# Moving the modulation's dot products in a two-layer trunk kernel: none amid layer 0's attention, the second norm's beside the output projections, the second gate's by columns in the down stage

## The chip, the cores and the metric

The kernel runs on one core of one Trainium2 chip. The metric is the device time of one execution in microseconds (us); less is better. The engines are TensorE (PE, matmuls; PEld is its loading of weights), VectorE (DVE), ScalarE (ACT), GpSimd (POOL) and SyncE (SP, which here issues most loads from HBM). Each engine works through its own instructions in order and waits at semaphores for the others.

## The reference

Two decoder layers over 512 tokens of 1024 channels, in float32. Six vectors per layer, made from a conditioning vector c, shift, scale and gate the two halves of a layer:

```python
mod = (c_act @ w_ada + b_ada)[:, None, :]
sh1, sc1, g1, sh2, sc2, g2 = jnp.split(mod, 6, axis=-1)
h = rmsnorm(x, norm1_w) * (1 + sc1) + sh1
u = h @ w_in                      # pool, conv, q/k/v and the gates' logits
...                               # pool mixer, short convolution, block-sparse attention
merged = (gates[:, :, 0] * (y_pool @ p_pool)
          + gates[:, :, 1] * (y_conv @ p_conv)
          + gates[:, :, 2] * (y_attn @ p_attn))
x = x + g1 * (merged @ w_out)
h2 = rmsnorm(x, norm2_w) * (1 + sc2) + sh2
x = x + g2 * ((jax.nn.silu(h2 @ w_gate) * (h2 @ w_up)) @ w_down)
```

So SC1 and SH1 are wanted at a layer's first norm, G1 at the output projections' residuals, SC2 and SH2 at the second norm, and G2 at the residuals of the down projection.

## The kernel before

Activations lie features by tokens: eight tiles (KT = 8) of 128 features x 512 tokens. Every product is made from split numbers. A float32 tile is divided into a high half (an ACT activation, `whi` for weights in L327, `big` for activations in L514) and a low half (a DVE subtraction, `wlo` in L330, `big` in L515), and `mm3` (L159) issues three matmuls per 128x128 block: high by high, high by low, low by high, which for an activation's use in a projection means: the weight's high half with the activation's high and low half, and the weight's low half with the activation's high half.

A layer runs in stages. First the input projections (L755 on); then attention with pool and convolution chains; then three sets of gates; then, in the order of the list `GATE2` (L75), the last gates and the attention's projection: a step `attn j` makes four block products into a PSUM bank, `gated` (L936, recorded as L938) multiplies them by the gate, L972 adds the other branches, and `split_from` (L510) splits the result into `merged[j]`. `tail` (L981) then runs the output projections: for each of the output columns n the eight merged tiles are multiplied by weight blocks, `residual` (L977, recorded as L978) scales the column by the modulation's gate and adds it to x, and the second norm's sums of squares are taken. Just ahead of `tail`, `table` (L172, recorded as L174) runs a one-column activation with the next function, ahead of which ACT loads the function's table. Then comes the feed-forward network in four parts (`PARTS`, L47): gate and up products, partly in pairs with fewer multiplications (`glu_pair`), followed by the part's down projection, again in eight columns with a residual each. Layer 0's part 3 ends with `tail` and layer 1's first norm.

A modulation vector is made of eight **dots**: one 512 KB tile of `w_ada` is loaded by SP, and one DVE instruction (`ada_dot`, L374, recorded as L376) multiplies it, 128x1024, by the activated c and accumulates a column of `mod`. `ada_end` (L405) adds the bias to all eight columns, and for SC1 and SC2 folds in the norm's weight. There are 96 dots. The 16 first ones are written out at the start; the others are queued as tasks in `bulk` by `ada_tasks` (L413).

What sets the order: a clock counted in matmul columns (`tick`, L135, called by `mm3`) runs queued tasks at `bulk_rate` per tick; `flush_bulk` runs all that are left and `drain` ends pending generators. So tasks take their place in the engines' orders when the program is built, between whatever is issued at that point. `ada_step` (L398) issues load and dot together; the tile comes from the pool tag `w4` (six slots, shared with the weights that POOL sums) or, with `early=True`, from `raw`, the ring of RAW = 3 tiles that weight loads use too. A load's issue waits on SP until the slot is free, and later loads wait behind it; a scheduler puts the issue of a load earlier than its dot.

Where the dots lie before the change:
- layer 0: SC2 and SH2 (`early`) amid the attention, at rate 0.27, the rest flushed after the last `attn` step; G2 in the output projections of both layers at rate 0.9;
- the next layer's vectors as list `later`, a part of it in each down stage of layer 0: `DOTS` = 8, 8 and 2 tasks in parts 0 to 2, five in part 3, and what is left in layer 1's first stage at rate 0.75 (L763 on).

Of the kernel before, what the change touches and what calls it, by code (L numbers as in the profile page):

```python
# [25 lines left out]
KT = D // P  # L26
# [21 lines left out]

SUMS_AHEAD = 4

DOTS = (8, 8, 2, 0)

RAW, BIG = 3, 46

# [25 lines left out]
def hybrid_trunk(ctx, tc, xT, ws, ada, cols, pool_w, qk_w, crow, pos, con, out):  # L80
# [50 lines left out]
    def flush_bulk():  # L131
        while bulk:
            bulk.popleft()[1]()
# [12 lines left out]
    def drain():  # L146
        while fibers:
            tick()
# [256 lines left out]
    def ada_end(l, part):  # L405
# [4 lines left out]
        if part == G1:  # L410
            V.tensor_scalar(m, m, 0.5, None, op0=ALU.mult)

    def ada_tasks(l, parts, early=False):  # L413
        out = []
        for part in parts:
            for j in range(KT):
                out.append((1.2, lambda part=part, j=j: ada_step(l, part, j, early)))
            out.append((0.2, lambda part=part: ada_end(l, part)))
        return out
# [320 lines left out]
    for l in range(L):  # L740
# [7 lines left out]
        for n, (k, lo, hi) in enumerate([(k, 0, S) for k in range(KT)] if l == 0 else HALVES + REST):  # L748
            if l == 0:
                if k + 3 < KT:  # L750
                    first.append(ada_first_load(k + 3))
                if k + 2 < KT:
                    ada_first(k + 2, first[k + 2], SC1)
                    ada_first(k + 2, first[k + 2], SH1)
                    norm.first_scaled(k + 2)  # L755
                    norm.first_hi(k + 2)
                loaded.append(load_w())
                if k + 2 < KT:
                    norm.first_lo(k + 2)
            if k not in held:  # L760
                held[k] = next_w(0 if l == 0 else None)
            if l > 0 and n == 1:
                second(norm, l, 0, bank)  # L763
                bulk.extend(later)
                bulk_rate[0] = 0.75
            w = held[k]
            h = norm.k(k)
            for t in range(lo // P, hi // P):
                mm3(q_ps[t], cut(h, slice(None), slice(t * P, (t + 1) * P)), wrow(w, 0), k == 0, k == KT - 1)
            for z in range(3):  # L770
                mm3(f_ps[z][:, lo:hi], wblk(w, 4 + z), cut(h, slice(None), slice(lo, hi)),
                    k == 0 and lo == 0, k == KT - 1)
# [148 lines left out]
            mm3(pp, (pw["h"][:, j, :], pw["l"][:, j, :]), pooled[j], True, True)  # L921
            y_pool.append(split_from(pp, scale=col(C_PS + j)))

        if l == 0:
            bulk.extend(ada_tasks(l, (SC2, SH2), True))
        bulk_rate[0] = 0.27
        ahead_now[0] = 3

        def gate():
# [29 lines left out]
        for step, j in GATE2:  # L959
            if step == "gate":  # L960
                sg2[j] = gate()
                continue
            if j == 0:
                drain()
            if j % 2 == 0:
                aw_ = next_w()
            p1 = ps_mm()
            for z in range(PAIRS):
                mm3(p1, wblk(aw_, 4 * (j % 2) + z), y_attn[z], z == 0, z == PAIRS - 1)
            t = sg2.pop(j)  # L970
            gated(t, p1)
            V.tensor_add(t, t, m01[j])  # L972
            merged.append(split_from(t))
        flush_bulk()


        def residual(k, src, lo, hi, part):  # L977
# [50 lines left out]
            return go  # L1028

        ahead_now[0] = 4  # L1030
        bulk.extend(ada_tasks(l, (G2,)))
        bulk_rate[0] = 0.9
        n2 = Norm()
        n2.h = [bigt(F32) for _ in range(KT)]
        table(AF.Abs_reciprocal_sqrt, t[:, 0:1])
# [41 lines left out]
        def glu_pair(last):  # L1077

            both = range(2)
            e = [ps_pair()[:, 0, :BLOCK] for _ in both]  # L1080
            a, c = [None] * 2, [None] * 2
            one, two = [None] * 2, [None] * 2
            w = [next_w() for _ in both]
            for z in both:
                group(e[z], w[z], 1, "B21", True)
            for z in both:
                a[z], one[z] = ps_mm()[:, :BLOCK], tmp()
                group(a[z], w[z], 0, "B11", True)
                C11 = one[z][:, :BLOCK]
                A.activation(C11, a[z], AF.Copy)  # L1090
                V.tensor_add(C11, C11, e[z])
            w = [next_w() for _ in both]
            for z in both:
                c[z], two[z] = ps_mm()[:, :BLOCK], tmp()
                group(c[z], w[z], 0, "R1", True)
                A.activation(two[z][:, BLOCK:], c[z], AF.Copy)
            for z in both:
                group(a[z], w[z], 1, "-V", False)
                A.activation(one[z][:, BLOCK:], a[z], AF.Copy)

            w = [next_w(2 if last else None) for _ in both]
            for z in both:
                group(c[z], w[z], 0, "B22", False)
                C12 = one[z][:, BLOCK:]
                V.tensor_add(C12, C12, c[z])
            for z in both:
                group(a[z], w[z], 1, "T3", False)
                m22 = two[z][:, BLOCK:]
                ins = V.tensor_add(m22, m22, a[z])
                if last:  # L1110
                    pin(ins)
            w = next_w(2 if last else None)
            for z in both:
                group(a[z], w, z, "T4", False)

            (g1, u1), (g2, u2) = one, two
            A.activation(g1, g1, AF.Silu)
            A.activation(g2[:, BLOCK:], g2[:, BLOCK:], AF.Silu, scale=-1.0)
            A.activation(g2[:, :BLOCK], a[0], AF.Silu, scale=-1.0)
            V.tensor_mul(u1, u1, g1)  # L1120
            act.append(split_from(u1))
            V.scalar_tensor_tensor(u2[:, BLOCK:], u2[:, BLOCK:], -1.0, g2[:, BLOCK:], op0=ALU.mult, op1=ALU.mult)
            V.scalar_tensor_tensor(u2[:, :BLOCK], a[1], -1.0, g2[:, :BLOCK], op0=ALU.mult, op1=ALU.mult)
            act.append(split_from(u2))
            dots_after[0] = last_split[0]

        for part, (along, single, pairs) in enumerate(PARTS):
            act = []
            nk = along + single + 2 * pairs
            if along:  # L1130
                held = {}
                for n, (k, lo, hi) in enumerate(HALVES + REST):
                    if n == 1:
                        second(norm, l, 1, bank)
                        table(AF.Silu, norm.y[:, 0:1])
                    if k not in held:
                        held[k] = next_w(3 if n == 0 else None)
                    for z in range(2 * FA):
                        mm3(f_ps[z][:, lo:hi], wblk(held[k], z), cut(norm.k(k), slice(None), slice(lo, hi)),
                            k == 0 and lo == 0, k == KT - 1)  # L1140
                    if k >= HK:
                        make_forms(k - HK)
                del held
                for z in range(FA):
                    glu(f_ps[z], f_ps[FA + z])
            for _ in range(single):
                wg = next_w()
                g = ps_mm()
                feature_tile(g, wg)
                u = ps_mm()  # L1150
                feature_tile(u, next_w())
                glu(g, u)
            bulk_rate[0] = 0.0
            for p in range(pairs):
                glu_pair(p == pairs - 1)
            if l + 1 < L:
                if part == 0:
                    later = ada_tasks(l + 1, (SC1, SH1, SC2, SH2))
                n = DOTS[part]
                bulk.extend(later[:n])  # L1160
                del later[:n]
            bulk_rate[0] = 1.5
            blk = Blocks(nk, 4)
            if part + 1 < len(PARTS):
                for n in range(KT):
                    if n == KT // 2:
                        bulk_rate[0] = 0.0
                    o = ps_mm()
                    for k in range(nk):
                        mm3(o, blk(n, k), act[k], k == 0, k == nk - 1)  # L1170
                    residual(n, o, 0, S, G2)
            elif l + 1 == L:
                tail(lambda k: act[k], blk, G2, nk, None, True)
            else:
                flush_bulk()
                drain()
                bulk.extend(later[:5])
                del later[:5]
                bulk_rate[0], credit[0] = 0.8, 0.0
                n1 = Norm()  # L1180
                table(AF.Abs_reciprocal_sqrt, f32(act[-1][1])[:, 0:1])
                scratch = ps_pair()
                bank = scratch[:, 1]
                tail(lambda k: act[k], blk, G2, nk, n1, False, lead(n1, l + 1, 0, bank), 4)
                norm = n1
# [100 lines left out]
```

## Time and profile before

| | us |
|---|---|
| median of three runs (lowest to highest) | 1452.05 (1451.97 to 1452.85) |
| profiled execution | 1453.0 |
| its span | 1451.2 |
| PE busy in the span | 1442.0 |
| DVE busy | 1063.1 |
| ACT busy | 663.5 |
| the 80 dots on `w4`, busy on DVE | 95.9 |

The clock granted to PE was 1.00 throughout. A row of the timeline gives the start in us, the duration, the engine, the line, the operation with its output and input, and how many instructions in a row it stands for (then the duration is from the first one's start to the last one's end); in brackets stand the idle time before it and what ended it. Instructions of one engine can overlap by a little: the next starts before the end of the one before. A row of the groups ends with busy time, mean, and the engine's idle time just before them with the releaser.

### The profile page before, as it was taken

The numbers are of one execution on the slowest core, as the hardware profiler recorded it, in microseconds if no ns is written. First come the engines' busy times: TensorE is split into PE (matmuls) and PEld (weight loads), VectorE is DVE, ScalarE is ACT, GpSimd is POOL, SyncE is SP. The second block draws the span as 40 slices with busy tenths as digits, with TensorE's granted clock in tenths as the row PEclk, the third lists the DMA queues.
The fourth block names the chain that finished last, engine by engine and source line by source line (L and its number), as shares of the span: only waits on it lengthen the run. The fifth ranks groups of instructions, "written<-read, shape, count | busy, mean of one in ns | idle before, by whom it ended". The sixth has DMA issues, their size and how long they took to land.

```text
span 1451.2 us, 21838 instructions
## 1 busy us (share of the span) xinstructions
PE 1442.0 (99%) x8379; PEld 1264.8 (87%) x8379; DVE 1063.1 (73%) x1879; ACT 663.5 (46%) x1138; POOL 105.2 (7%) x157
## 2 busy tenths in 40 slices
PE   9999999999999999999999999999999999999998
PEld 7888788888988998989988877888889989989997
DVE  7987888858686767677797776776577757657663
ACT  4634555533553452535444355555335525534450
POOL 0000000001100311210000000000020102111200
PEclk9999999999999999999999999999999999999999
DMA  9644333364436767756545422223473436636432
GB/s 352 223 141 167 124 115 104 117 217 152 100 132 213 196 174 205 187 153 195 190 147 178 151 87 73 73 73 109 153 200 90 135 113 175 174 106 185 131 92 83
DMA packets 84409, 217.18 MB, mean 150 GB/s; under 512 B 10832, under 2 KB 23760, under 8 KB 84304
## 3 DMA queue, kind: packets, MB, share of 16 engines
q1 hardware_dynamic: 67456, 177.37, 35.9%
q0 software_dynamic: 16128, 37.76, 11.8%
q8 instruction: 65, 1.06, 0.3%
q10 hardware_dynamic: 720, 0.66, 0.1%
q14 instruction: 40, 0.33, 0.1%
HBM read 213.65 MB, written 2.10 MB: 149 GB/s over the span
## 4 chain that ended last, share of the span: by engine, by line
PE 92%; DVE 5%; DMA 1%; ACT 1%; issue 1%; SPq 0%; ACTq 0%; DVEq 0%
PE mm L151 78%; PE pair L151 12%; PE mm L157 1%; DVE wlo L330 1%; DMA w<-in_ada 1%; DVE w L376 0%; DVE raw L376 0%; DMA x<-in_xT 0%; DMA raw<-in_ws 0%; DVE tmp L643 0%; DVE asm L622 0%; ACT tmp L638 0%; DVE asm L629 0%; DVE asm L623 0%; ACT tmp L635 0%
## 5 line engine op out<-in xcount | busy, mean ns | idle before, releaser
L151 PE MATMUL mm<-big,whi 128*128 128x512 f32 (+1 forms) x4362 | 1080.2, 339 | 1.7 <-DVE big L938 0.9
L151 PEld LDWEIGHTS mm<-big,whi 128*128 128x128 f32 x4362 | 745.2, 190 | 87.2 <-DVE big L938 1.5
L151 PE MATMUL mm<-big,wlo 128*128 128x512 f32 (+1 forms) x2181 | 736.1, 338 | 0.0
L151 PEld LDWEIGHTS mm<-big,wlo 128*128 128x128 f32 x2181 | 413.8, 190 | 44.5
L327 ACT ACTIVATE whi<-raw 128x1024 fp32r<-128x1024 f32 (+2 forms) x240 | 248.9, 1040 | 265.7 <-PE mm L151 190.2
L330 DVE TENSOR_TENSOR wlo<-raw,whi 128x1024 fp32r<-128x1024 f32 (+2 forms) x240 | 283.9, 1192 | 50.5 <-ACT whi L327 47.7
L327 ACT ACTIVATE whi<-w 128x1024 fp32r<-128x1024 f32 x72 | 76.2, 1058 | 148.1 <-PE mm L151 85.3
L978 DVE SCALAR_TENSOR_TENSOR x<-mm,mod,x 128x512 f32<-128x512 f32 (+1 forms) x90 | 61.7, 689 | 78.1 <-PE mm L151 77.9
L256 POOL DMA_DIRECT2D w<-in_ws x72 | 46.3, 656 | 951.6 <-issue 294.1
L330 DVE TENSOR_TENSOR wlo<-w,whi 128x1024 fp32r<-128x1024 f32 x72 | 86.7, 1221 | 31.6 <-ACT whi L327 30.9
L376 DVE SCALAR_TENSOR_TENSOR w<-w,csil 128x1024 f32<-128x1024 f32 x80 | 95.9, 1220 | 16.9 <-DMA w<-in_ada 16.8
L151 PE MATMUL pair<-whi,big 128*128 128x512 f32 x224 | 76.8, 390 | 0.0
L258 POOL DMA_DIRECT2D w<-in_ws x72 | 64.0, 897 | 157.8 <-DMA w<-in_ws 142.6
L151 PE MATMUL pair<-big,whi 128*128 128x256 f32 (+1 forms) x376 | 74.0, 294 | 0.0
L151 PEld LDWEIGHTS pair<-big,whi 128*128 128x128 f32 x376 | 60.4, 191 | 2.2
L151 PE MATMUL mm<-whi,big 128*128 128x512 f32 x160 | 57.2, 394 | 1.4 <-ACT big L501 1.1
L151 PE MATMUL pair<-big,wlo 128*128 128x256 f32 (+1 forms) x188 | 55.3, 294 | 0.0
L938 DVE SCALAR_TENSOR_TENSOR big<-big,mm 128x512 f32<-128x512 f32 x48 | 32.5, 683 | 28.6 <-PE mm L151 28.5
L151 PEld LDWEIGHTS pair<-whi,big 128*128 128x128 f32 x224 | 42.1, 188 | 8.8
L515 DVE TENSOR_TENSOR big<-tmp,big 128x512 fp32r<-128x512 f32 x48 | 33.1, 691 | 21.4 <-ACT big L514 20.4
L514 ACT ACTIVATE big<-tmp 128x512 fp32r<-128x512 f32 x48 | 29.9, 622 | 36.2 <-DVE tmp L1120 12.8
L151 PE MATMUL pair<-wlo,big 128*128 128x512 f32 x112 | 43.6, 390 | 0.0
(190 smaller groups left out, 1238.5 us busy)
## 6 DMA issues: line engine op xcount, KB each, us to landing
raw<-in_ws SPq DMA_DIRECT2D x146, 512.0 KB, 3.3
w<-in_ada SPq DMA_DIRECT2D x80, 512.0 KB, 4.9
w<-in_ws POOLq DMA_DIRECT2D x144, 256.0 KB, 4.7
raw<-in_ws SPq DMA_DIRECT2D x64, 256.0 KB, 3.8
raw<-in_ws SPq DMA_DIRECT2D x24, 384.0 KB, 3.5
raw<-in_ada SPq DMA_DIRECT2D x16, 512.0 KB, 3.3
raw<-in_ws SPq DMA_DIRECT2D x16, 448.0 KB, 5.1
raw<-in_ws SPq DMA_DIRECT2D x36, 128.0 KB, 2.8
```

Source lines behind the costliest of these rows:

```text
L151: tc.keep_in_program_order(T.matmul(*a, **k))
L157: tc.keep_in_program_order(T.transpose(*a))
L256: nc.gpsimd.dma_start(dst, self.source(0, 1))
L258: nc.gpsimd.dma_start(dst, self.source(*other), accum_op=ALU.add)
L327: A.activation(hi[:, :n], raw[:, :n], AF.Copy)
L330: ins = V.tensor_sub(lo[:, :n], raw[:, :n], f32(hi)[:, :n])
L376: return V.scalar_tensor_tensor(aw, aw, 1.0, csil, op0=ALU.mult, op1=ALU.mult, accum_out=mod[l][:, part, j:j + 1])
L514: A.activation(hi, src, AF.Copy)
L515: last_split[0] = V.tensor_sub(lo, src, f32(hi))
L938: V.scalar_tensor_tensor(sg, sg, 1.0, branch, op0=ALU.add, op1=ALU.mult)
L978: V.scalar_tensor_tensor(x[k][:, lo:hi], src, mod[l][:, part, k:k + 1], x[k][:, lo:hi], op0=ALU.mult, op1=ALU.add)
```

## The change

- `DOTS` becomes (0, 9, 4, 0), and `later` holds only SC1 and SH1 of the next layer: part 0's down stage of layer 0 has none of the next layer's tasks, parts 1 and 2 have nine and four, part 3 what is left (five), and layer 1's first stage none.
- No dots are queued amid layer 0's attention (rate 0). In both layers SC2's and SH2's tasks are queued at the first `attn` step, at rate 0.85 and on the `w4` ring; the flush after the last `attn` step goes, so that what is left runs on into the output projections, where `tail` flushes it.
- G2's tasks in the output projections go. Instead `g2_column` makes one column of G2: its load, its dot, and a one-column ACT activation that adds the bias. In part 0's down stage of both layers three columns are made ahead of the loop over the output columns and column n + 3 at the top of iteration n, so that four stand ahead of the first column's products.

In the resulting order, DVE has four dots in a row behind the split of the last pair's product and ahead of the three splits of down weights that followed it before. Between `attn 4` and `attn 7` two dots stand on DVE: one between the low halves of merged tiles 4 and 5, one behind the next weight tile's low half. On ACT the table load and its one-column activation stand between the high halves of merged tiles 6 and 7, in both layers; before, they stood behind both. PE's order is the same instruction by instruction. Lines behind L413 move by two to seven: L514/L515 become L520/L521, L938 becomes L940, L972 becomes L976, L978 becomes L981.

```diff
-DOTS = (8, 8, 2, 0)
+DOTS = (0, 9, 4, 0)
...
+    def g2_column(l, j):
+
+        ada_step(l, G2, j, False)
+        m = mod[l][:, G2, j:j + 1]
+        A.activation(m, m, AF.Identity, bias=colt[:, l, C_ADA + G2 * KT + j:C_ADA + G2 * KT + j + 1])
...
             if l > 0 and n == 1:
                 second(norm, l, 0, bank)
-                bulk.extend(later)
-                bulk_rate[0] = 0.75
...
-        if l == 0:
-            bulk.extend(ada_tasks(l, (SC2, SH2), True))
-        bulk_rate[0] = 0.27
+        bulk_rate[0] = 0.0
...
             if j == 0:
                 drain()
+                bulk.extend(ada_tasks(l, (SC2, SH2)))
+                bulk_rate[0] = 0.85
...
             merged.append(split_from(t))
-        flush_bulk()
...
         ahead_now[0] = 4
-        bulk.extend(ada_tasks(l, (G2,)))
-        bulk_rate[0] = 0.9
...
                 glu_pair(p == pairs - 1)
+            if part == 0:
+                for j in range(3):
+                    g2_column(l, j)
             if l + 1 < L:
                 if part == 0:
-                    later = ada_tasks(l + 1, (SC1, SH1, SC2, SH2))
+                    later = ada_tasks(l + 1, (SC1, SH1))
...
                     if n == KT // 2:
                         bulk_rate[0] = 0.0
+                    if part == 0 and n + 3 < KT:
+                        g2_column(l, n + 3)
...
-                bulk.extend(later[:5])
-                del later[:5]
+                bulk.extend(later)
                 bulk_rate[0], credit[0] = 0.8, 0.0
```

## The prediction

> **What bounds the kernel now.** I read the page first: the span, the engines, the chain of work that ended last, the dots and their loads; its last row here is from the view of the dots' operand (us of DVE's idle time, times).
>
> ```profile
> span 1451.2 us, 21838 instructions
> PE 1442.0 (99%) x8379; PEld 1264.8 (87%) x8379; DVE 1063.1 (73%) x1879; ACT 663.5 (46%) x1138; POOL 105.2 (7%) x157
> PE 92%; DVE 5%; DMA 1%; ACT 1%; issue 1%; SPq 0%; ACTq 0%; DVEq 0%
> L376 DVE SCALAR_TENSOR_TENSOR w<-w,csil 128x1024 f32<-128x1024 f32 x80 | 95.9, 1220 | 16.9 <-DMA w<-in_ada 16.8
> w<-in_ada SPq DMA_DIRECT2D x80, 512.0 KB, 4.9
> ...
> DMA w<-in_ada: 16.8, 14
> ```
>
> TensorE (PE) is busy for 1442.0 of 1451.2 us, and 92% of the chain is its own matmuls. The change touches none of them: PE runs the same matmuls in the same order in both kernels. So only PE's waits can change, and the second question is how much waiting there is to win. I asked for PE's waits in the stretch of layer 0's attention (which has dots amid it) and in the same stretch of layer 1 (which has none), and for both stretches' busy times.
>
> ```profile
> PE mm L157 <- DVE tmp L672: 0.6, 1, 0.6
> PE mm L151 <- ACT big L933: 0.4, 1, 0.4
> ...
> PE mm L151 <- DVE big L938: 0.9, 1, 0.9
> PE mm L157 <- DVE big L909: 0.3, 1, 0.3
> ...
> 120.00:300.00 180.00, 179.06 (x924) 146.64 (x923) 149.00 (x347) 93.47 (x214) 0.00 (x0) 1.00 0.36 121
> 835.00:1015.00 180.00, 178.39 (x919) 145.44 (x918) 130.89 (x314) 95.26 (x216) 0.00 (x0) 1.00 0.24 82
> ```
>
> The first two rows are all of layer 0's waits, 1.0 us; the next two are the larger ones of layer 1 (columns: total, times, longest). In the windows the columns are length, then busy PE, PEld, DVE, ACT, POOL. Without dots, layer 1's VectorE (DVE) is busy 18 us less, and PE still idles 1.61 us there against 0.94 us with them.
>
> **The change, part by part.** One dot occupies DVE for 1.22 us; in a row they start 1.145 us apart (455.11 and 456.25 below). The number of dots and of their 512 KB loads does not change; their places do.
>
> *Layer 0's attention loses 16 dots* (19.5 us of DVE, 16 loads on SP's queue and raw ring). At most the 1.0 us of waits can go, so the bounds are 0 and −1.0. Layer 1's idle PE without dots (1.61 against 0.94) says near 0: the wait at L672 is followed by the softmax's own chain. I take −0.2. The raw ring then serves weights alone; they come earlier, and PE waits for none there now: nothing.
>
> *SC2's and SH2's 16 dots go to the steps around the last gates and the attention projections and into the output projections of both layers, where G2's 8 were.* This is the part that costs. The new order of DVE has two dots among the last four merged tiles: one between the low halves of merged tiles 4 and 5, one behind the next weight tile's low half. And the order of ScalarE (ACT) changes: the table load of the next norm stands between the high halves of tiles 6 and 7, where now it follows both. The rows of now, layer 0: DVE, ACT, PE.
>
> ```profile
> 335.38 1.37 DVE L515 TENSOR_TENSOR big<-big,big 128x512 fp32r<-128x512 f32 x2
> 336.67 1.22 DVE L330 TENSOR_TENSOR wlo<-raw,whi 128x1024 fp32r<-128x1024 f32 x1
> 337.80 0.68 DVE L938 SCALAR_TENSOR_TENSOR big<-big,mm 128x512 f32<-128x512 f32 x1
> 339.38 0.69 DVE L938 SCALAR_TENSOR_TENSOR big<-big,mm 128x512 f32<-128x512 f32 x1 [0.17 <-PE mm L151]
> 340.82 1.37 DVE L515 TENSOR_TENSOR big<-big,big 128x512 fp32r<-128x512 f32 x2
> ...
> 340.17 1.29 ACT L514 ACTIVATE big<-big 128x512 fp32r<-128x512 f32 x2
> 341.48 1.28 ACT L174 ACT_TABLE_LOAD   x1
> 342.78 0.20 ACT L174 ACTIVATE tab<-big 128x1 f32<-128x1 f32 x1
> ...
> 343.26 0.62 PE L151 MATMUL mm<-big,whi 128*128 128x512 f32 x2
> 343.94 0.62 PE L151 MATMUL mm<-big,whi 128*128 128x512 f32 x2
> ```
>
> PE's two rows are the first output column's use of merged tiles 6 and 7. The two whi matmuls of a row take first the high, then the low half, 0.23 us later (three matmuls fill the 0.68 us from row to row): high 6 is due at 343.26, low 6 at 343.49, high 7 at 343.94, low 7 at 344.17. Now the low halves end at 342.19, 1.98 us before low 7 is due. Now the same with the new order, each start 0.08 us before the end of an independent instruction before it:
> - DVE: low 4 335.38 to 336.07; dot to 337.21; low 5 to 337.82; weight's low half to 338.96; dot to 340.10. The two L938 of tiles 6 and 7 end at 340.70 and 341.31 (they began at 337.80 and 339.38), the two additions (0.69 each) at 341.92 and 342.54.
> - ACT: high 6 from 341.95, half of 1.29, to 342.59; table load 1.28 to 343.89; the one-column activation 0.20 to 344.10; high 7 to 344.70.
> - DVE: low 7 from 344.73 to 345.42.
> Low 7 is due at 344.17, so PE waits 345.42 − 344.17 = 1.25 us; overlap of the small activation with high 7 may take 0.1 off: 1.2. Low 6 ends at 343.30, 0.19 us ahead. Neither the dots nor the load does it alone: without the load high 7 would start at 342.59 and low 7 end near 343.9, 0.25 us in time; without the dots the load would end before it mattered.
>
> Layer 1 has the same order and the same distances:
>
> ```profile
> 1055.30 0.69 DVE L938 SCALAR_TENSOR_TENSOR big<-big,mm 128x512 f32<-128x512 f32 x1 [0.18 <-PE mm L151]
> 1056.73 1.37 DVE L515 TENSOR_TENSOR big<-big,big 128x512 fp32r<-128x512 f32 x2
> ...
> 1057.40 1.28 ACT L174 ACT_TABLE_LOAD   x1
> ...
> 1059.86 0.62 PE L151 MATMUL mm<-big,whi 128*128 128x512 f32 x2
> ```
>
> 1055.30 − 339.38 = 715.92 and 1059.86 − 343.94 = 715.92: another 1.2 us. Sum of the part: +2.4, with bounds 0 (dots a quarter microsecond quicker, load hidden) and, if both dots wait for their loads as the 14 waits of the dots now do, 16.8/14 = 1.2 us each time, one such wait more in each layer: +2.4 + 2.4 = +4.8. A load lands in 4.9 us and is issued when an earlier dot leaves one of the ring's six slots, several dots ahead, so I take +2.4. Behind it the output projections hold five dots ahead of SH2's end instead of eight; the residuals have two PSUM banks of time, and the next norm's application comes after all columns: nothing. If that cover went, a dot's 1.22 us.
>
> On the table load a page speaks against the change. The Trainium skill, ScalarE: Activation LUTs, section "What ACT_TABLE_LOAD costs", gives about 1283 ns for the load and another 1380 ns or so for a drain at each switch. The rows agree on the load (1.28) and show no drain: it starts 0.02 us after the high halves end (341.46) and the next activation 0.02 us after it.
>
> *G2 by columns in the down stage of part 0, both layers.* Four dots stand behind the last pair's split and ahead of three splits of down weights, then one a column; 16 one-column ACT instructions (0.20 each by the row of 342.78, 3.2 us on an engine 46% busy) replace two additions.
>
> ```profile
> 451.70 3.48 DVE L330 TENSOR_TENSOR wlo<-raw,whi 128x1024 fp32r<-128x1024 f32 x3
> 455.11 1.22 DVE L376 SCALAR_TENSOR_TENSOR w<-w,csil 128x1024 f32<-128x1024 f32 x1
> 456.25 1.22 DVE L376 SCALAR_TENSOR_TENSOR w<-w,csil 128x1024 f32<-128x1024 f32 x1
> 457.40 0.74 DVE L978 SCALAR_TENSOR_TENSOR x<-mm,mod,x 128x512 f32<-128x512 f32 x1
> ...
> 461.06 0.39 PE L151 MATMUL mm<-big,wlo 128*128 128x512 f32 x1
> ...
> 1167.62 3.59 DVE L330 TENSOR_TENSOR wlo<-raw,whi 128x1024 fp32r<-128x1024 f32 x3
> ...
> 1176.98 0.39 PE L151 MATMUL mm<-big,wlo 128*128 128x512 f32 x1
> ```
>
> The first of the three splits ends at 452.92 and PE takes it at 461.06; in layer 1 1168.84 and 1176.98: 8.14 us of slack each. Four dots take 4 × 1.145 = 4.6, so 3.5 us remain: nothing. The first residual comes at 456.3 + 3.5 = 459.8 instead of 457.4, and waits for its column of G2, which is then there; its PSUM bank is next wanted more than a column (18 matmuls of 0.68/3 us, 4.1 us) later. The last four dots come one a column; their loads wait in SP's queue for a dot's slot, with the weights' loads behind them. If they make weights late, PE waits (below).
>
> *The rest.* Layer 0's parts 1 and 2 have 9 and 4 dots instead of 8 and 2, behind their splits; part 3 has 4 and SH1's end instead of 5; layer 1's first stage loses 11. PE waits for none of these now: nothing either way, bounds −0.3 (the 0.3 of L909) and +1.2 (one dot in the way).
>
> *Sum:* −0.2 + 1.2 + 1.2 = +2.2 us. The profiled execution took 1453.0 us (span 1451.2), so 1455.2; the median of the three runs, 1452.05, lies 0.95 lower, which gives 1454.3.
>
> **Rivals.**
> 1. *Hidden.* No wait at the table load: the two low halves have a margin of 1.0 us to find in a chain of some ten handovers, or a dot of the two falls behind. With up to 1.0 us won in attention, 1452.05 − 0.5 = 1451.5. For it: 0.25 us decides once the load is away. Against it: the order puts the load before high 7, and 1.28 + 0.20 exceeds what remains.
> 2. *Slower by more than 0.2%: the four dots ahead of part 0's splits.* The place is 451.70 (and 1167.62), the price begins when they take over 3.5 us longer than 4.6. If each waits 1.2 us for its load, as the 14 waits now, 4.8 − 3.5 = 1.3 us is lost per layer: 1454.3 + 2.6 = 1456.9. For it: SP's queue holds two of their loads behind weight loads. Against it: these wait for splits that ended long before.
> 3. *A longer switch.* A drain at the two loads, as the page has it, as a delay of high 7. The nearest row of that size here is a table load itself, so 1.28 more in each layer: 1454.3 + 2.6 = 1456.9. By the page's own 1.38 it would be 1457.1. Against it: the two gaps of 0.02 us.
> 4. *Faster by over 0.2%.* All avoidable waits of layer 0's attention are 1.0 us, and 2.9 us would be needed: hardly possible, unless the DMA traffic moved out of attention frees time that no wait shows.
>
> **How the numbers follow.** 0.2% is 2.9 us, about what a measurement of this kernel can tell from no change. The stall at both loads, +1.5 to +2.9: 0.45. Hidden: 0.14, nearly all within 0.2%. The two rivals of 2.6 us more and a dot late at the loads: 0.23, 0.03 and 0.11, together 0.37, nearly all slower by over 0.2%. Faster: 0.04. Of the likeliest case a tenth lies above +2.9. So faster 0.04, same 0.55, slower 0.41. The likeliest case's own range is 1453.5 to 1455.0; with the others 1451.4 (hidden) to 1457.4 (second rival and a late dot).
>
> **What would show it.** PE's waits would name an L521 release of merged tile 7 with about 1.2 us, once near 344 and once near 1060; ACT's timeline would have the load between two L520 instructions. Layer 0's attention would keep a wait at L672 or L940. No PE wait would lie in 452 to 500 or 1168 to 1216. I am wrong if the waits near 344 are under 0.5 us, if there is one in the down stage, or if PE's busy time itself moves by over 1 us.

## The result, and the profile after

The changed kernel took 1454.93 us in the median of 21 runs (1454.49 to 1456.81), the kernel before 1452.24 (1451.52 to 1453.43); the ratio is 1.0019, with a 95% interval of 1.0012 to 1.0026. So it is 2.7 us slower, against 2.2 us (1454.3) forecast, inside the range and just inside the 0.2% called no change.

The profiled execution of the changed kernel took 1456.81 us, the longest of the 21. The first lines of its page and PE's waits in the whole span (total, times, longest):

```profile
span 1455.0 us, 21854 instructions
PE 1444.0 (99%) x8379; PEld 1266.0 (87%) x8379; DVE 1062.0 (73%) x1877; ACT 668.6 (46%) x1154; POOL 105.4 (7%) x157
...
PE mm L151 <- ACT big L507: 1.5, 1, 1.5
...
PE mm L151 <- ACT big L520: 1.1, 2, 0.6
...
PE mm L157 <- ACT big L935: 0.8, 1, 0.8
PE mm L151 <- DVE big L521: 0.4, 2, 0.2
```

New in it are the waits for L520 and L521, the high and the low half of a merged tile, twice each, and one for L935. Here are the steps around the table load of layer 0: ACT, DVE, then PE; and PE in layer 1.

```profile
343.87 0.64 ACT L520 ACTIVATE big<-big 128x512 fp32r<-128x512 f32 x1 [1.67 <-DVE big L976]
344.52 1.28 ACT L174 ACT_TABLE_LOAD   x1
345.82 0.20 ACT L174 ACTIVATE tab<-big 128x1 f32<-128x1 f32 x1
345.93 0.61 ACT L520 ACTIVATE big<-big 128x512 fp32r<-128x512 f32 x1
...
341.95 1.28 DVE L940 SCALAR_TENSOR_TENSOR big<-big,mm 128x512 f32<-128x512 f32 x2
343.15 1.29 DVE L976 TENSOR_TENSOR big<-big,big 128x512 f32<-128x512 f32 x2
344.54 0.69 DVE L521 TENSOR_TENSOR big<-big,big 128x512 fp32r<-128x512 f32 x1
346.58 0.69 DVE L521 TENSOR_TENSOR big<-big,big 128x512 fp32r<-128x512 f32 x1 [1.34 <-ACT big L520]
...
345.66 0.39 PE L151 MATMUL mm<-big,wlo 128*128 128x512 f32 x1
346.60 0.50 PE L151 MATMUL mm<-big,whi 128*128 128x512 f32 x1 [0.55 <-ACT big L520]
347.32 0.50 PE L151 MATMUL mm<-big,whi 128*128 128x512 f32 x1 [0.22 <-DVE big L521]
...
1063.33 0.50 PE L151 MATMUL mm<-big,whi 128*128 128x512 f32 x1 [0.55 <-ACT big L520]
1064.06 0.50 PE L151 MATMUL mm<-big,whi 128*128 128x512 f32 x1 [0.22 <-DVE big L521]
```

High 7 starts 2.06 us after high 6, because the load and the small activation stand between them; low 7 follows at 346.58, and PE, which has nothing else to do, waits for each half. Since PE's order is the same in both kernels, each of its matmuls can be laid beside the same one of before, and the difference of their starts tells where time is lost and won:

```
stretch, us in the trace of before     offset of the changed kernel at its end   gained or lost
start to 132                           +1.94                                     +1.94
layer 0's attention, to 309            +1.94                                      0.00  (+0.32 at 141, -1.35 at 162, +0.91 at 248, and small ones)
gates, output projections, to 370      +3.28                                     +1.34  (1.21 of it at the two halves of merged tile 7)
feed-forward of layer 0, to 783        +3.26                                     -0.02
to 844 (at 838 to 840)                 +2.71                                     -0.55
layer 1's attention, to 1022           +2.76                                     +0.05
output projections, to 1083            +4.13                                     +1.37  (again 1.21 at merged tile 7)
to the end                             +4.15                                     +0.02
```

The 1.94 us at the start and the −0.55 near 840 belong to these two executions, not to the change: the third experiment below starts with the same instructions as the changed kernel, and its offset at 132 is 0.21. Of the 1.94, PE had lost 1.39 by the matmul at 17.89, most of it in two waits (for a DVE result at 12, for an ACT result at 18). Then the clock fell: the granted clock between 20 and 24 us was 0.57 in this execution and 1.00 in that experiment's. The offset rose to 2.93 meanwhile, and came back to 1.86 by 33 us, so the clock's part is about 0.5. (Windows: length, busy time of PE, PEld, DVE, ACT and POOL, clock, DMA share, GB/s; the first row is the changed kernel's, the second that experiment's.)

```profile
20.00:24.00 4.00, 3.88 (x11) 3.07 (x11) 3.54 (x7) 0.89 (x4) 0.00 (x0) 0.57 1.01 399
```

```profile
20.00:24.00 4.00, 4.00 (x18) 2.77 (x16) 3.52 (x5) 1.34 (x3) 0.00 (x0) 1.00 1.03 405
```

The −0.55 shows in most other executions against this one of before, also in that of the second experiment, where the order there is the one of before (0.54). What remains are the two places of the table load, 1.34 + 1.37 = 2.71 us, against 2.69 between the medians. That these agree to 0.02 us is chance, since the interval of the ratio alone is 2 us wide.

### The profile page after: what moved, and what is told of

Its sections match the earlier page's. It is cut to its first block, busy times and chain, and to the rows that moved or that the text cites. A ratio compares the mean times of both kernels' runs of the same rounds, so it can differ in the third digit from the quotient of the medians.

```text
span 1455.0 us, 21854 instructions
## 1 busy us (share of the span) xinstructions
PE 1444.0 (99%) x8379; PEld 1266.0 (87%) x8379; DVE 1062.0 (73%) x1877; ACT 668.6 (46%) x1154; POOL 105.4 (7%) x157
## 3 DMA queue, kind: packets, MB, share of 16 engines
q8 instruction: 65, 1.06, 0.3%
## 5 line engine op out<-in xcount | busy, mean ns | idle before, releaser
L376 DVE SCALAR_TENSOR_TENSOR w<-w,csil 128x1024 f32<-128x1024 f32 x96 | 115.1, 1220 | 11.9 <-DMA w<-in_ada 11.9
L981 DVE SCALAR_TENSOR_TENSOR x<-mm,mod,x 128x512 f32<-128x512 f32 (+1 forms) x90 | 61.4, 688 | 70.9 <-PE mm L151 70.8
L521 DVE TENSOR_TENSOR big<-tmp,big 128x512 fp32r<-128x512 f32 x48 | 33.0, 690 | 21.0 <-ACT big L520 19.9
L520 ACT ACTIVATE big<-tmp 128x512 fp32r<-128x512 f32 x48 | 29.9, 624 | 34.8 <-DVE tmp L1121 12.8
L940 DVE SCALAR_TENSOR_TENSOR big<-big,mm 128x512 f32<-128x512 f32 x48 | 32.4, 684 | 13.7 <-PE mm L151 13.5
```

Of the source, the lines that this page charges most:

```text
L376: return V.scalar_tensor_tensor(aw, aw, 1.0, csil, op0=ALU.mult, op1=ALU.mult, accum_out=mod[l][:, part, j:j + 1])
L520: A.activation(hi, src, AF.Copy)
L521: last_split[0] = V.tensor_sub(lo, src, f32(hi))
L940: V.scalar_tensor_tensor(sg, sg, 1.0, branch, op0=ALU.add, op1=ALU.mult)
L981: V.scalar_tensor_tensor(x[k][:, lo:hi], src, mod[l][:, part, k:k + 1], x[k][:, lo:hi], op0=ALU.mult, op1=ALU.add)
```

## The experiments

In the expectations, theory A is that of the prediction: the two dots and the place of the load together make PE wait.

**The load behind both high halves.** Only what the small activation reads is changed, so that it, and with it the load, comes after high 7; DVE's and PE's orders stay as they were.

```diff
-        table(AF.Abs_reciprocal_sqrt, t[:, 0:1])
+        table(AF.Abs_reciprocal_sqrt, f32(merged[-1][0])[:, 0:1])
```

> The changed kernel with one difference: the table load of the second norm stands behind the high half of merged tile 7 instead of between those of tiles 6 and 7; the order of DVE and PE is the same. Theory A (the two dots and the place of the load together make PE wait, 1.2 us in each layer): high 7 follows high 6 at once and low 7 ends some 0.2 us before PE wants it, so both waits go and the time falls by 2.4 us, from 1454.9 to about 1452.5. Theory B (the place of the load alone does it): the same 1452.5. Theory C (the two dots alone do it): the waits of about 1.2 us stay, 1454.9. Theory D (the 2.7 us lie elsewhere, at the start or in the attention, and the waits at the load are made up later): the waits go and the time stays near 1454.9.

Measured: 1452.28 us beside 1452.37 for the kernel before, ratio 1.0000 (0.9991 to 1.0009). Its ACT, DVE and PE near the load:

```profile
342.86 1.23 ACT L520 ACTIVATE big<-big 128x512 fp32r<-128x512 f32 x2 [1.67 <-DVE big L976]
344.11 1.28 ACT L174 ACT_TABLE_LOAD   x1
...
343.52 1.29 DVE L521 TENSOR_TENSOR big<-big,big 128x512 fp32r<-128x512 f32 x2
...
344.64 0.39 PE L151 MATMUL mm<-big,wlo 128*128 128x512 f32 x1
344.87 0.62 PE L151 MATMUL mm<-big,whi 128*128 128x512 f32 x2
```

Both high halves run in a row and PE goes on without a gap: low 7 ends at 344.81, 0.3 us ahead of 344.87 + 0.23 (the prediction had 0.25). Laid beside the changed kernel, PE gains 1.33 us here and 1.35 in layer 1, and nothing later takes it back. So theory D falls (the time lies elsewhere), and C (the dots alone).

**The load between the high halves, in the kernel before.** The call is moved to a line ahead of the last split.

```diff
+            if j == 7:
+                table(AF.Abs_reciprocal_sqrt, t[:, 0:1])
             merged.append(split_from(t))
...
-        table(AF.Abs_reciprocal_sqrt, t[:, 0:1])
```

> The kernel before with the table load of the second norm between the high halves of merged tiles 6 and 7, and no dots moved. Theory A: by the rows of before high 6 ends at 340.82, the load at 342.12, the small activation at 342.32, high 7 near 342.9 and low 7 near 343.6, 0.6 us before 344.17: no wait, 1452.2 as before. Theory B: waits of 1.2 us in each layer, 1454.6. Theory C: no wait, 1452.2.

Measured: 1453.01 us beside 1452.37, ratio 1.0004 (0.9995 to 1.0013).

```profile
340.74 1.28 ACT L174 ACT_TABLE_LOAD   x1
...
342.14 0.62 ACT L514 ACTIVATE big<-big 128x512 fp32r<-128x512 f32 x1
...
342.79 0.69 DVE L515 TENSOR_TENSOR big<-big,big 128x512 fp32r<-128x512 f32 x1 [1.35 <-ACT big L514]
...
343.87 0.62 PE L151 MATMUL mm<-big,whi 128*128 128x512 f32 x2
```

The load stands where the change puts it, and PE has no wait: low 7 ends at 343.48, 0.6 us ahead of 343.87 + 0.23. Theory B (the load alone) falls.

**The load between, without the two dots.** The changed kernel, with the load's call ahead of the last split as above and the tasks held from `attn 4` until the output projections.

```diff
+            if j == 4:
+                bulk_rate[0] = 0.0
...
         ahead_now[0] = 4
+        bulk_rate[0] = 0.85
```

> The changed kernel with the load where the change has it (between the high halves), but without the two dots between the last four merged tiles: the tasks stop at attn 4 and go on in the output projections. Theory A: no wait, the time falls by 2.4 us to about 1452.5. Theory B: the waits of 1.2 us in each layer stay, 1454.9. Theory C: no wait, 1452.5.

Measured: 1452.63 us beside 1452.37, ratio 0.9998 (0.9989 to 1.0007). Its DVE and PE:

```profile
343.00 0.69 DVE L521 TENSOR_TENSOR big<-big,big 128x512 fp32r<-128x512 f32 x1 [1.35 <-ACT big L520]
...
344.08 0.62 PE L151 MATMUL mm<-big,whi 128*128 128x512 f32 x2
```

Low 7 ended at 343.69, and PE took it at 344.08 + 0.23 without a wait. With the three runs the four combinations are complete: dots alone (the first run), no wait; load alone (the second, and this one), no wait; neither (the kernel before), none; both, 1.2 us in each layer.

**One dot more.** The changed kernel with three dots there instead of two.

```diff
+            if j == 6:
+                bulk.popleft()[1]()
```

> The changed kernel with one dot more between the last four merged tiles (three instead of two, taken from the same queue), the load between the high halves of tiles 6 and 7 as the change has it. If the wait is the plain sum of what stands on DVE and ACT ahead of low 7 (theory A), each dot adds its 1.145 us to the 1.21 us: waits of about 2.35 us in each layer and 1454.9 + 2.3 = 1457.2. If the dots only fill idle time (theory C wrong way round: the load sets the wait), it stays at 1.2 us and 1454.9.

Measured: 1458.07 us beside 1453.20, ratio 1.0035 (1.0021 to 1.0049); against the changed kernel's 1.0019 that is 2.3 us more. Layer 1 is what the sum says: 1.12 us more than the changed kernel by PE's offsets. PE waits in it for both halves of tiles 6 and 7, the same in both layers:

```profile
PE mm L151 <- ACT big L520: 0.9, 2, 0.6
PE mm L151 <- DVE big L521: 0.5, 2, 0.2
```

In layer 0 the profiled execution, the longest of the five at 1459.56 us, lost 1.5 us beyond that 1.2; what it shows there is told at the end.

**All eight columns ahead.** For the four dots ahead of the down splits the prediction forecast no cost, with 3.5 us left. This run uses that up.

```diff
-                for j in range(3):
+                for j in range(KT):
                     g2_column(l, j)
...
-                    if part == 0 and n + 3 < KT:
-                        g2_column(l, n + 3)
```

> The changed kernel with all eight columns of G2 ahead of the first column's products in part 0's down stage, instead of four. The prediction gave the first down split 8.14 us of slack. Eight dots take 9.16 us, so PE should wait 1.0 us in each layer: 1456.9. Rival: the last two loads need the slots of the first two dots, and stand in SP's queue ahead of weights; if they or the weights come late, the waits are several us: over 1458. Second rival: the slack is larger than the rows say and nothing is seen: 1454.9.

Measured: 1458.43 us beside 1453.20, ratio 1.0036 (1.0024 to 1.0049), 2.5 us above the changed kernel by the ratios. PE's offsets against the changed kernel give +1.09 and +1.08 at one matmul of each layer, 1.26 with the slower matmuls just behind it, and no other loss of that size. DVE and PE of layer 0, with the last dot and the three splits behind it:

```profile
462.16 1.23 DVE L376 SCALAR_TENSOR_TENSOR w<-w,csil 128x1024 f32<-128x1024 f32 x1
...
463.30 3.49 DVE L330 TENSOR_TENSOR wlo<-raw,whi 128x1024 fp32r<-128x1024 f32 x3
...
464.58 0.50 PE L151 MATMUL mm<-big,wlo 128*128 128x512 f32 x1 [0.92 <-DVE wlo L330]
```

The eight dots run without a gap, so no load was late, and PE waits for the first split: the slack read from the rows, 8.14 us, is right to 0.1 us.

**No dots amid layer 0's attention.** The kernel before without those 16 dots; it leaves out their product, and their columns stay zero ahead of the bias.

```diff
-            bulk.extend(ada_tasks(l, (SC2, SH2), True))
+            V.memset(mod[0][:, SH2:SC2 + 1], 0.0)
+            ada_end(l, SC2)
+            ada_end(l, SH2)
```

> The kernel before without the 16 dots of layer 0's SC2 and SH2 (left out, their columns are zero, so the second norm's scale and shift of layer 0 lack their product; bias and folding stay). It measures what the dots amid layer 0's attention cost. My reading of the changed kernel's trace: the waits near 162 us (1.35 us in all) go, and others of about 1.2 us come further on in the attention because the order of ACT changes there, so that the net is -0.1 us, 1452.1. Rival: the gain of 1.35 us is the dots' price and the loss further on belongs to another part of the change: 1450.9. Second rival: nothing moves at all, since the waits are the softmax chain's own.

Measured: 1451.93 us beside 1452.37, ratio 0.9997 (0.9988 to 1.0006). The same three steps as in the changed kernel: +0.31 at 141, −1.35 at 162, +0.88 at 248. So they come from the dots' absence alone. PE's waits in the attention that remain are two, at 248 and at 141:

```profile
PE mm L157 <- ACT big L935: 0.7, 1, 0.7
PE mm L157 <- DVE tmp L643: 0.2, 1, 0.2
```

The step at 141 is again the place of a table load. ACT's rows of before, then of this run:

```profile
132.77 1.28 ACT L933 ACT_TABLE_LOAD   x1
...
139.31 0.46 ACT L616 ACTIVATE tmp<-pair,asm,nrq 128x128 f32<-128x128 f32 x1 [1.29 <-DVE asm L614]
```

```profile
139.39 1.28 ACT L616 ACT_TABLE_LOAD   x1
140.68 0.46 ACT L616 ACTIVATE tmp<-pair,asm,nrq 128x128 f32<-128x128 f32 x1
```

Before, a gate (L933) came first on ACT, and its load ran in idle time; the exponentials of the softmax (L616) behind it needed no load of their own. Without the dots the exponentials come ahead of that gate, and the load stands right in front of them. They start 1.37 us later, where PE is 1.06 us later in this trace, and the 0.31 between the two is the step. The changed kernel has the same order, its load at 140.26.

At 162 the gain comes from DVE, which without the dots reaches that softmax earlier. The same reduction before (behind a dot at 145.44) and in this run:

```profile
152.96 0.68 DVE L622 TENSOR_REDUCE asm<-pair 128x2 f32<-128x512 f32 x1
```

```profile
152.47 0.69 DVE L622 TENSOR_REDUCE asm<-pair 128x2 f32<-128x512 f32 x1 [0.83 <-PE pair L151]
```

In this run PE's starts are 1.39 us later there, yet DVE is ready and waits for it; before, DVE was behind, and PE then waited for L672 and a gate. ACT's rows tell the step at 248:

```profile
245.11 0.56 ACT L635 ACTIVATE tmp<-pair,asm,nrq 128x256 f32<-128x256 f32 x1
...
247.29 0.87 ACT L654 ACTIVATE w<-mm 128x384 fp32r<-128x384 f32 x2
248.03 0.62 ACT L935 ACTIVATE big<-mm 128x512 f32<-128x512 f32 x1
```

The first row is the first of four exponentials of a softmax, which run until 247.3; the two copies of another unit's transposed weights (L654) and a gate (L935) stand behind them, and PE's next transposes wait for the gate. With the dots, DVE was later with that softmax (its first L631 for it at 246.34 instead of 244.04), and the copies stand first, as ACT's rows of before show; that the lateness is why the scheduler chose so is argued, not shown:

```profile
245.01 0.88 ACT L654 ACTIVATE w<-mm 128x384 fp32r<-128x384 f32 x2 [1.22 <-PE mm L157]
...
247.46 0.55 ACT L635 ACTIVATE tmp<-pair,asm,nrq 128x256 f32<-128x256 f32 x1
```

**Dots amid the attention, but later.** The kernel of the first experiment with the 16 dots of layer 0 back amid the attention, from the third or second step of the gates on.

```diff
+            if l == 0 and j == 2:
+                bulk.extend(ada_tasks(l, (SC2, SH2), True))
+                bulk_rate[0] = 0.4
             s0, s1 = gate(), gate()
...
-                bulk.extend(ada_tasks(l, (SC2, SH2)))
+                flush_bulk()
+                bulk.extend(ada_tasks(l, () if l == 0 else (SC2, SH2)))
```

> The kernel with the load behind both high halves, and SC2's and SH2's dots of layer 0 put back amid the attention on the ring of weights, but from the third step of the gates on, at rate 0.4. If the dots before 162 us cost the 1.35 us there and the dots after it keep ACT's order near 248 us as it was before, both gains stand: 1452.3 - 1.2 = 1451.1. Rival: another order of ACT makes another wait of about 1 us: 1452.3.

> As the run before, from the second step of the gates on and at rate 0.27. The same two outcomes: 1451.1, or 1452.3 where the order of ACT turns elsewhere.

The first: 1452.15 us beside 1453.20, ratio 0.9993 (0.9985 to 1.0002). Its dots run from 168.9 on. It keeps the −1.35 at 162 and has no step at 248; a new one of 0.35 stands at 184. The second (`j == 1`, rate 0.27): 1457.93, ratio 1.0035 (1.0022 to 1.0047). Four of its dots stand between 151.2 and 157.3, ahead of the softmax near 160, and PE waits there, then once more near 308:

```profile
PE mm L157 <- DVE tmp L649: 2.0, 1, 2.0
PE mm L151 <- ACT big L679: 1.6, 1, 1.6
```

Neither outcome written down for it was that bad. The first and the kernel with the load behind were run again together.

> The same kernel as e7_late_dots a second time, since its interval just touched 1. If the 1.0 us that its trace showed against the kernel before holds, the ratio is again near 0.9993 and both together lie below 1; if it was chance, near 1.0000.

> The kernel of e1_load_last a second time, on the same chip as the run before: it shows what the place of SC2's and SH2's dots of layer 0 is worth with the load out of the way. Theory: 1.0 us above the run before. Rival: the same time.

Measured: 1452.55, ratio 0.9999 (0.9991 to 1.0008), and 1452.54, ratio 0.9997 (0.9988 to 1.0006), beside 1452.92. The gain of 1 us did not hold; this time the trace had a step of 0.99 us at 177. No version here beats the kernel before by more than the runs can tell.

## Why the prediction came out as it did

- *What bounds the kernel.* PE's order is the same and only its waits changed: right; the steps in the attention and at the loads are all waits of PE, with slower matmuls just behind them.
- *The dots and the table load, +1.2 us in each layer.* Right in mechanism and size: 1.21 at the two halves of merged tile 7, 1.34 and 1.37 with the slower matmuls just behind a wait (0.50 instead of 0.39). Moved by the 1.94 us by which this execution was late at that point, the forecast chain stands in the trace to 0.1 us: high 6 at 341.95 + 1.94 = 343.89 (343.87 measured), low 7 at 344.73 + 1.94 = 346.67 (346.58). The claim that neither does it alone held in each of the three runs made for it.
- *The load and the drain.* The page "ScalarE: Activation LUTs" of the Trainium skill has a drain of 1.38 us at a switch (section "What ACT_TABLE_LOAD costs"). The trace does not agree: the load starts 0.01 us after high 6 ends (344.51) and the small activation 0.02 us after the load. The rival that rested on it is out.
- *The attention, −0.2.* The number came close by luck; the reason was wrong. The prediction held that the wait at L672 was the softmax's own and that no more than 1.0 us could be won. In fact 1.35 us went at 162 when the dots went, since DVE had come late into that softmax; and 1.2 us came back at 141 and 248 through ACT's new order, which the prediction did not look at in this stretch. Net 0.0. The two listed waits, 1.0 us together, were also short of the 1.35 us that PE lost there.
- *G2 by columns, nothing.* Right: the changed kernel has no PE wait between 440 and 500 or 1168 and 1216, the four dots run in a row, and the first of the three splits ends (459.92 + 1.22 = 461.14) 3.2 us before PE wants it; 3.5 were forecast. The rival of late loads is out: no dot here waited, and even eight in a row did not. DVE and PE of the changed kernel:

```profile
455.34 1.22 DVE L376 SCALAR_TENSOR_TENSOR w<-w,csil 128x1024 f32<-128x1024 f32 x1
...
459.92 3.49 DVE L330 TENSOR_TENSOR wlo<-raw,whi 128x1024 fp32r<-128x1024 f32 x3
...
464.34 0.39 PE L151 MATMUL mm<-big,wlo 128*128 128x512 f32 x1
```

- *The rest, nothing.* Right to 0.02 us in layer 0's feed-forward.
- *The signs.* The load stands between two L520 rows, and the down stage has no wait, as foretold. Three signs came otherwise. PE's wait at merged tile 7 is not one release by L521: it stops first for the high half (0.55, L520) and then for the low half (0.22, L521), and the rest of the 1.21 is in the matmuls behind a wait, recorded as 0.50 us instead of 0.39. Layer 0's attention kept no wait at L672 (L678 in the changed kernel) or L940. And PE's busy time moved by 2.0 us (1442.0 to 1444.0), which was named as a sign of being wrong, though PE runs the same 8379 matmuls. That sign was badly chosen: the 49 matmuls from 338.06 to 348.72 before were busy 10.66 us, the same 49 from 340 to 352 in the changed kernel 11.23, so each stalled place adds 0.6 by itself; most of the rest stands at the start, where the clock fell.
- *The sum.* 2.2 us forecast, 2.7 measured (interval 1.7 to 3.8). The 0.5 between them lies within the interval; by the trace it is the 0.15 us in each layer of slower matmuls behind the waits, and the 0.2 us that the attention did not give.

## What to carry to other kernels

Two delays that are each hidden can cost together: add up everything that stands on each engine ahead of the one result that is wanted next, and compare it with the slack of that result alone. A table load is safer behind the last instruction that feeds the bounding engine than between the last two: between them it was free here only while no dots stood ahead on DVE. When work moves off an engine, the order of the other engines can change too, table loads included, so look at it in the stretch that lost the work, even where the bounding engine's order is unchanged.

## What the runs showed of the hardware that was not expected

With three dots, PE in layer 0 waited four times within 3.4 us, none longer than 0.6 us and 1.4 us in all; right behind it the granted clock fell, and the matmuls from 348.15 to 351.14 started 0.43 us apart instead of 0.23, which makes most of the 1.5 us that this execution lost there. In layer 1, after the same four waits, the clock stayed at 1.00. The windows of that kernel, layer 0's and layer 1's:

```profile
347.00:349.50 2.50, 2.27 (x7) 1.55 (x7) 2.50 (x3) 1.06 (x1) 0.54 (x1) 0.69 0.95 152
349.50:352.00 2.50, 2.50 (x9) 2.00 (x8) 2.50 (x6) 0.00 (x0) 0.57 (x1) 0.62 0.87 243
...
1067.00:1070.00 3.00, 3.00 (x14) 2.47 (x15) 3.00 (x3) 1.06 (x1) 0.00 (x0) 1.00 0.81 141
```

The length of the waits does not decide it: in the second run with late dots PE waited 2.0 us in one piece up to 164.04 and 0.5 more up to 168.30, and the clock stayed at 1.00:

```profile
164.00:168.00 4.00, 3.80 (x18) 2.80 (x18) 3.95 (x12) 2.73 (x5) 0.00 (x0) 1.00 0.02 6
```

What decides was not tried, and that the short waits made the clock fall is not shown either. The Trainium skill, TensorE: Matmul & The Clock Gate, Part 1, has the clock fall after an idle window of about 3.4 us and calls the window free-running. Here no idle stretch was near that long, and in layer 0 the clock fell all the same.
